# Operands 256 bytes apart within 512, a staging pool beside the first phase, and an early router, in a transformer layer on one core

## The chip, the cores and the metric

The kernel runs on one core of one Trainium2 chip, in one launch. The metric is the device time of that core in microseconds; beside it stands the span, the time between the first and the last instruction of one profiled execution.

## The reference, cut to what matters

Everything is float32, batch 1, 1024 tokens of width 1024. Two blocks follow each other; the first has an attention and convolution mixer and a mixture of experts, the second a recurrent branch (HGRN) and a forgetting attention (FOX).

```
mod = silu(c) @ w_ada + b_ada                     # sh1, sc1, g1, sh2, sc2, g2; the same for the 256 context tokens
xn = rmsnorm(x) * (1 + sc1) + sh1                 # and xn_c of the context
q, k, v, gb, gc, xc = split(xn @ w_in)            # rope on q and k; context keys and values ahead
attn = head_out((softmax(q0 k0) - lam softmax(q1 k1)) @ v)
conv = gb * conv3(gc * xc)
h = x + g1 * rmsnorm(concat(attn, conv) @ w_out)
xn = rmsnorm(h) * (1 + sc2) + sh2
aff = softmax(xn @ w_router)                      # 16 experts
g, idx = top_k(aff.T, 128)                        # each expert takes its 128 best tokens
ff = scatter_add(idx, (silu(xn[idx] @ w_gate) * (xn[idx] @ w_up)) @ w_down * g)
h = h + g2 * rmsnorm(ff)
# second block: u = rmsnorm(h); y = concat(hgrn(u), fox(u)); h += y @ w_out_2
# h += sigmoid(h @ w_ple_gate_2) * (p @ w_ple_2); out = rmsnorm(h)
```

## The kernel before, in words

Every large product is made of three. A float32 operand is split into a high part, rounded to the type fp32r, and a low part, the rest: ACT casts the high part (L82) and VectorE subtracts (L83). `mm3` then adds high x high, high x low and low x high (L77 to L79). In the rows the operand that streams (the moving one) is named first behind the arrow, the one loaded into the array (the stationary one) second. A product has 128 rows, 128 columns of the stationary operand, and 512 or 256 columns of the moving one.

Tiles lie in pools. A pool is a stretch of each partition's memory; pools of the left side are stacked from the low end, those opened with `side="right"` from the high end, in the order in which they are opened. The place of a tile is therefore the sum of the sizes ahead of it. Nearly all tiles are multiples of 512 bytes; a few small ones (`sg`, 4 bytes; `idxT` and `gT`, 64 bytes each; `mx`, `sm`, `r` of 24 and 8 bytes; `cu`, 4104 bytes) set the residue of all that lie behind them. By these sums the residues modulo 512 in this kernel are: pools on the right (`xn`, `wo`, `mw`, `uT`, `wk`) 480; `cx` and `pw` (context and qkv weights) 224; in attention K, Q and V 224, a 0 and the conv weights 32; in the output projection `mh` and `ml` 96; the MoE's `xs`, hidden rows and `ml`, HGRN's and FOX's `pj`, and the last projection's `finw`, `finy` and `finl` 352.

The work follows in stages, by the profile: modulation and the projections to q, k, v (to 268 us); attention, with the convolution's products between its steps (to 578); the output projection with the router, `phase2` and `mixed` (to 694); the experts' choice of tokens (to 775); the MoE (to 1360); the second block's normalization, HGRN, FOX and the last projection.

In `phase0`, eight blocks of `w_ada` of 1 MB come through three buffers of `pw`; VectorE accumulates the first 512 columns over the context's and the tokens' vector, PE makes the rest. `A1` (L213) ends this. Then 256 context tokens and two groups of 512 tokens are normalized, transposed, and written as `ch`/`cl`, `xn[0]` and `xn[1]`. `qkv` opens the pool `pA` only after `phase0`'s pool `p0` is closed, so its tiles (`cos`, `sin`, the staging tiles `sth` and `stl`, and rope's) lie where `p0` lay, and the first instruction to use such a tile waits for those that used the place before.

In `phase2`, `mixed` runs for eight blocks of 128 tokens: output projection, two RMS norms (`rstd` is Ln and Exp on ACT), then `xn` by two operations on VectorE (L613, L614), eight transposes, logits, softmax into `af`. The first MoE weight blocks are loaded during this (`next_raw`). `ple` follows, a small product for the end, then `choose`: 16 rounds of MAX8, FIND_INDEX8 and MATCH_REPLACE8 over the affinities. The MoE's weights come as 192 blocks of 1 MB; `block` casts and splits them in order into `mw` (four of six) or `ml` (two of six). The first `PB` = 4 are subtracted on POOL, `NR` = 6 raw buffers are in flight. A scheduler sets the order of each engine's instructions when the program is built, by priority and free tiles, and each engine then executes its own in that order; `issue_after` in the change adds a bound to it.

```
hi, lo = self.block()
for k in range(2):
    for n in range(2):
        matmul(ps[n], xh[:, i, :], hi[:, k, c])   # stationary, moving
```

Of the kernel before, what the change touches and what calls it, by code (L numbers as in the profile page):

```python
# [19 lines left out]
P = 128  # L20
D = 1024
# [28 lines left out]
class Kernel:  # L50
# [16 lines left out]


# [22 lines left out]
    def constants(self, st):  # L91
# [18 lines left out]
        self.sg = self.t(c, [P, 1], F32, "sg")  # L110
# [20 lines left out]
    def phase0(self):  # L131

        nc, I = self.nc, self.I
        with ExitStack() as st:
# [4 lines left out]
            def load(src, r0):  # L139
                x = self.t(p, [P, D], F32, "x", bufs=7)  # L140
                nc.sync.dma_start(x, src[r0:r0 + P, :])
                xs.append(x)

            def wa(cb, kh):
                w = self.t(self.pw, [P, 4, 512], F32, "raw", bufs=3)
                nc.sync.dma_start(w, I["w_ada"][0, kh * 512:(kh + 1) * 512, cb * 512:(cb + 1) * 512].rearrange("(k p) c -> p k c", p=P))
# [3 lines left out]
            order = ((1, 0), (0, 0), (1, 1), (2, 0), (0, 1), (2, 1), (3, 0), (3, 1))  # L150
# [3 lines left out]
            for b in range(2):  # L154
                load(I["ctx"][0], b * P)
# [10 lines left out]
            nc.vector.tensor_tensor(self.sc.rearrange("p k v -> p v k"), e, cv, op=ALU.mult)  # L166
# [3 lines left out]
            nc.vector.tensor_tensor(pr, lvv[:, :, 0, :], lvv[:, :, 1, :], op=ALU.mult)  # L170
# [8 lines left out]
            tm = self.t(self.pp, [P, 512], F32, "mm", bufs=4)  # L179
            acc = [self.t(p, [P, 512], F32, f"acc{v}") for v in range(2)]  # L180
            ps = None
            for i, (cb, kh) in enumerate(order):
                w = was[i]
                if i + 3 < len(order):
                    was.append(wa(*order[i + 3]))
                if cb == 0:
                    for k in range(4):
                        for v in range(2):
                            s = self.sc[:, kh * 4 + k, v:v + 1]
                            if kh + k == 0:  # L190
                                nc.vector.tensor_scalar(acc[v], w[:, k, :], s, None, op0=ALU.mult)
                            else:
                                nc.vector.scalar_tensor_tensor(acc[v], w[:, k, :], s, acc[v], op0=ALU.mult, op1=ALU.add)
                    if kh == 0:
                        continue
                    for j in range(4):
                        for v in range(2):
                            nc.tensor.matmul(tm[:, 2 * j + v:2 * j + v + 1], acc[v][:, j * P:(j + 1) * P], self.onec, start=True, stop=True)
                    continue
                if kh == 0:  # L200
                    ps = self.t(self.pp, [P, 512], F32, "mm", bufs=4)
                for k in range(4):
                    nc.tensor.matmul(ps[:2, :], self.sc[:, kh * 4 + k, :], w[:, k, :], start=(kh * 4 + k == 0), stop=(kh * 4 + k == 7))
                if kh == 1:
                    m2 = self.t(p, [2, 512], F32, "m2", bufs=2)
                    nc.vector.tensor_copy(m2, ps[:2, :])
                    for j in range(4):
                        c = 2 * (cb * 4 + j)
                        nc.tensor.transpose(tm[:, c:c + 2], m2[:, j * P:(j + 1) * P], self.ident[:2, :2])
            md = self.t(p, [P, 16, 2], F32, "md")  # L210
            nc.vector.tensor_tensor(md, tm[:, :32].rearrange("p (j v) -> p j v", v=2), VC[:, 16:32].unsqueeze(2).broadcast_to([P, 16, 2]), op=ALU.add)
            nc.vector.tensor_copy(self.SH1, md[:, 0:8, :])
            nc.vector.scalar_tensor_tensor(self.A1, md[:, 8:16, :], 1.0, VC[:, 32:40].unsqueeze(2).broadcast_to([P, KB, 2]), op0=ALU.add, op1=ALU.mult)  # L213

            raws = [self.wraw(512, kh) for kh in range(2)]
            for b in range(8):
                load(I["x"][0], b * P)
            for v, g, blks in ((1, 0, xs[0:2]), (0, 0, xs[2:6]), (0, 1, xs[6:10])):
# [7 lines left out]
                for k in range(KB):  # L226
                    tp = self.t(pp, [P, 512], F32, "tp", bufs=3)
                    for b, x in enumerate(blks):
                        nc.tensor.transpose(tp[:, b * P:(b + 1) * P], x[:, k * P:(k + 1) * P], self.ident)
                    tt = self.t(p, [P, 512], F32, "tt", bufs=2)  # L230
                    nc.scalar.activation(tt[:, :n], tp[:, :n], AF.Identity, scale=self.A1[:, k, v:v + 1], bias=self.SH1[:, k, v:v + 1])
                    hi, lo = (self.ch, self.cl) if v else self.xn[g]
                    if k % 2:
                        nc.scalar.copy(hi[:, k, :], tt[:, :n])
                    else:
                        nc.vector.tensor_copy(hi[:, k, :], tt[:, :n])
                    nc.vector.tensor_tensor(lo[:, k, :], tt[:, :n], f(hi[:, k, :]), op=ALU.subtract)
                if v:
                    self.W = [self.wsplit(r) for r in raws]


    def phase1(self):
        nc, I = self.nc, self.I
        with ExitStack() as st:
            self.stx = ExitStack()
            xp = self.pool(self.stx, "xn", side="right")
            self.xn = [(self.t(xp, [P, KB, 512], F32R, f"xh{g}"), self.t(xp, [P, KB, 512], F32R, f"xl{g}")) for g in range(2)]
            with ExitStack() as st2:
# [3 lines left out]
                self.pw = self.pool(st2, "pw")  # L252
                self.pp = self.pool(st2, "pAp", 2, space=PSUM)
# [4 lines left out]
    def qkv(self, st):  # L258
# [5 lines left out]
        self.cos = self.t(w, [P, SEQ], F32, "cos")  # L264
        self.sin = self.t(w, [P, SEQ], F32, "sin")
        nc.sync.dma_start(self.cos, I["k_cos"])
        nc.sync.dma_start(self.sin, I["k_sin"])
        wsl = lambda W, c: [(W[k // 4][0][:, k % 4, c], W[k // 4][1][:, k % 4, c]) for k in range(KB)]
        groups = ((0, CTX, (self.ch, self.cl)), (CTX, 512, self.xn[0]), (CTX + 512, 512, self.xn[1]))
        for base, dst in ((512, self.K_d), (0, self.Q_d)):  # L270
            W = self.W if base else self.win(0)
            for c0, n, x in groups[0 if base else 1:]:
                for h in range(HEADS):
# [3 lines left out]
                    hi = self.t(w, [P, 512], F32R, "sth", bufs=2)  # L277
                    lo = self.t(w, [P, 512], F32R, "stl", bufs=2)
# [8 lines left out]
            if base:  # L287
                W = self.win(1024)
                for b in range(10):
# [3 lines left out]
                    hi = self.t(w, [P, 512], F32R, "sth", bufs=2)  # L293
                    lo = self.t(w, [P, 512], F32R, "stl", bufs=2)
# [13 lines left out]
    def wraw(self, c0, kh):  # L308
        raw = self.t(self.pw, [P, 4, 512], F32, "raw", bufs=3)
# [44 lines left out]
    def rope(self, ps, t0, scale, hi, lo):  # L354

        nc, w = self.nc, self.wp
# [54 lines left out]
    def scores(self, i):  # L411
        nc, w, pp = self.nc, self.wp, self.pp
        h, b = divmod(i, 8)
        if b == 0:
# [18 lines left out]
        mx = self.t(w, [P, 2, 3], F32, "mx", bufs=3)  # L433
        sm = self.t(w, [P, 2, 3], F32, "sm", bufs=3)
# [54 lines left out]
    def conv(self, cb, which, g, w, bufs, early=False):  # L489
        nc = self.nc  # L490
        if which == 0 and g == 0:
            u = self.t(w, [P, SEQ + 2], F32, "cu", bufs=1)
# [5 lines left out]
        if g == 0:  # L498
            def tile(dt, tag):
                if not early:  # L500
                    return self.t(w, [P, KB, P], dt, tag, bufs=2)
                return self.t(self.pw, [P, 4, 512], dt, tag, bufs=3)[:, 0:2, :].rearrange("p a (b c) -> p (a b) c", c=P)
# [37 lines left out]
    def phase2(self):  # L540

        nc, I = self.nc, self.I
        with ExitStack() as st:
# [8 lines left out]
            affT = self.t(w, [2 * NE, 512], F32, "affT")  # L552
            self.raws = []
# [6 lines left out]
            for i in range(8):  # L560
# [24 lines left out]
    def mixed(self, w, pp, tb, wo, G1, SH2, A2, wr, af):  # L585
# [27 lines left out]
        nc.vector.scalar_tensor_tensor(xn, x, s2[:, 3:4], A2, op0=ALU.mult, op1=ALU.mult)  # L613
        nc.vector.tensor_tensor(xn, xn, SH2, op=ALU.add)  # L614
        nc.scalar.dma_start(self.xn2_d[t, :], xn)
        xT = self.t(w, [P, KB, P], F32, "xT", bufs=1)
        for kh in range(2):
            tp = self.t(pp, [P, 512], F32, "tp")
            for k in range(4):
                nc.tensor.transpose(tp[:, k * P:(k + 1) * P], xn[:, (kh * 4 + k) * P:(kh * 4 + k + 1) * P], self.ident)  # L620
# [4 lines left out]
        r4 = self.t(w, [P, 4], F32, "r4", bufs=2)  # L625
        nc.vector.tensor_reduce(r4[:, 0:1], lg[:, :NE], axis=AX.X, op=ALU.max)
        nc.vector.tensor_scalar(r4[:, 1:2], r4[:, 0:1], -1.0, None, op0=ALU.mult)
        nc.scalar.activation(af, lg[:, :NE], AF.Exp, bias=r4[:, 1:2], accum_out=r4[:, 2:3])
        nc.vector.reciprocal(r4[:, 3:4], r4[:, 2:3])
        nc.vector.tensor_scalar(af, af, r4[:, 3:4], None, op0=ALU.mult)  # L630
# [84 lines left out]
    def block(self):  # L715
# [5 lines left out]
        return self.hlrows(self.mw if (self.nb - 1) % 6 < 4 else self.ml, raw, self.nc.gpsimd if self.nb <= PB else None)  # L721
# [503 lines left out]
    def fox_scores(self, h, tb):  # L1225
# [28 lines left out]
        sm = self.t(w, [P, 2], F32, "sm", bufs=6)  # L1254
# [244 lines left out]
```

## Time and profile before

| what | value |
|---|---|
| median of 3 runs | 2869.68 us (2868.32 to 2872.84) |
| the profiled execution | 2866.51 us, span 2864.7 us |
| mean granted clock | 0.967 |
| PE busy | 2645.4 us (92%), 14213 matmuls |
| VectorE (DVE) busy | 2002.0 us (70%) |
| ScalarE (ACT) busy | 1624.9 us (57%) |
| GpSimd (POOL) busy | 247.7 us (9%) |
| DMA | 516.43 MB, mean 180 GB/s |

A matmul's busy time covers its passage through the array, and the next one starts before it ends; the distance from start to start tells what one costs in a dense row. A releaser in brackets ("4.22 <-DVE stl L83") gives the idle time of the engine ahead of an instruction and what ended it.

### The profile page before, as it was taken

The page shows a single profiled execution, that of the slowest core. Times are in us where ns is not written, and L with a number is a line of the kernel's source. Part 1 is how long each engine was busy: PE and PEld are TensorE (multiplying, and loading weights), DVE is VectorE, ACT ScalarE, POOL GpSimd, SP SyncE. Part 2 cuts the span into 40 slices and gives each one's busy share as a digit, 9 for nine tenths or more (in the row PEclk, how much of TensorE's full clock was granted, in tenths as well). Part 3 has the DMA queues.
Part 4 walks back from the last instruction along what each step waited for, and adds up shares of the span by engine and source line. Part 5 has one row for each costly group of instructions (what it writes and reads, how often), then busy time and mean ns, then how long its engine had stood idle before and what let it go on. Part 6 is the DMA issues. An engine that isn't in the chain of part 4 may idle for free.

```text
span 2864.7 us, 38667 instructions
## 1 busy us (share of the span) xinstructions
PE 2645.4 (92%) x14213; PEld 2205.3 (77%) x14213; DVE 2002.0 (70%) x3287; ACT 1624.9 (57%) x2858; POOL 247.7 (9%) x344
## 2 busy tenths in 40 slices
PE   7899999887699999999599999998999998989998
PEld 3677887776588877777489999997878786777776
DVE  5864998845688888887557767673777676776535
ACT  5212898734377777776545545543666665774335
POOL 0101000003000000000100000000111110230000
PEclk9999999998799999999799999999999999999999
DMA  7767333256399999998612122226665766475612
GB/s 283 233 208 197 94 87 90 71 189 228 144 373 375 365 365 370 368 354 280 231 46 52 45 44 46 38 72 161 177 162 139 164 161 139 136 192 190 201 59 81
DMA packets 309090, 516.43 MB, mean 180 GB/s; under 512 B 52529, under 2 KB 180094, under 8 KB 308900
## 3 DMA queue, kind: packets, MB, share of 16 engines
q1 hardware_dynamic: 291628, 456.04, 51.3%
q0 software_dynamic: 11136, 36.25, 4.4%
q10 hardware_dynamic: 6136, 21.67, 2.0%
q8 instruction: 112, 1.84, 0.3%
q14 instruction: 78, 0.64, 0.1%
HBM read 421.01 MB, written 92.88 MB: 179 GB/s over the span
## 4 chain that ended last, share of the span: by engine, by line
PE 54%; DMA 7%; ACT 6%; DVE 3%; issue 2%; SPq 0%; POOL 0%; DVEq 0%; ACTq 0%; POOLq 0%
PE mm L77 9%; PE mm L79 9%; PE mm L78 9%; PE av L1300 2%; PE pu L732 2%; PE pu L733 2%; PE pu L731 2%; PE pg L732 2%; PE py L732 2%; PE py L733 2%; PE py L731 2%; PE pg L733 2%; PE pg L731 2%; PE sc L1021 2%; PE tp L1291 1%
## 5 line engine op out<-in xcount | busy, mean ns | idle before, releaser
L83 DVE TENSOR_TENSOR wlo<-raw,whi 128x2048 fp32r<-128x2048 f32 (+1 forms) x280 | 542.0, 1963 | 167.5 <-ACT whi L82 163.6
L82 ACT CAST whi<-raw 128x2048 fp32r<-128x2048 f32 (+1 forms) x284 | 459.4, 1653 | 142.3 <-PE mm L78 65.2
L77 PE MATMUL mm<-uh,whi 128*128 128x512 f32 x640 | 258.6, 404 | 0.9 <-ACT uh L793 0.9
L78 PE MATMUL mm<-ul,whi 128*128 128x512 f32 x640 | 256.2, 400 | 0.0
L79 PE MATMUL mm<-uh,wlo 128*128 128x512 f32 x640 | 255.3, 399 | 0.0
L79 PE MATMUL mm<-whi,ul 128*128 128x256 f32 x768 | 220.5, 287 | 0.0
L77 PE MATMUL mm<-whi,uh 128*128 128x256 f32 x768 | 220.2, 287 | 0.0
L78 PE MATMUL mm<-wlo,uh 128*128 128x256 f32 x768 | 217.6, 283 | 0.0
L77 PEld LDWEIGHTS mm<-whi,uh 128*128 128x128 f32 x768 | 145.4, 189 | 0.2
L79 PEld LDWEIGHTS mm<-whi,ul 128*128 128x128 f32 x768 | 145.5, 189 | 0.1
L78 PEld LDWEIGHTS mm<-wlo,uh 128*128 128x128 f32 x768 | 145.3, 189 | 0.2
L1269 ACT ACTIVATE lg<-lg,sm 128x128 f32<-128x128 f32 (+7 forms) x128 | 99.5, 777 | 80.4 <-DVE sm L1268 79.7
L79 PEld LDWEIGHTS mm<-uh,wlo 128*128 128x128 f32 x640 | 121.8, 190 | 26.1
L77 PEld LDWEIGHTS mm<-uh,whi 128*128 128x128 f32 x640 | 121.9, 191 | 24.7 <-ACT uh L793 1.4
L442 ACT ACTIVATE e<-sc,mx 128x512 f32<-128x512 f32 (+1 forms) x192 | 118.3, 626 | 39.1 <-DVE mx L441 38.2
L78 PEld LDWEIGHTS mm<-ul,whi 128*128 128x128 f32 x640 | 122.2, 191 | 23.7
L77 PE MATMUL mm<-xh,whi 128*128 128x512 f32 x320 | 128.6, 402 | 5.6 <-DVE stl L83 4.2
L79 PE MATMUL mm<-xh,wlo 128*128 128x512 f32 x320 | 127.2, 397 | 0.0
L78 PE MATMUL mm<-xl,whi 128*128 128x512 f32 x320 | 126.9, 397 | 0.0
L1300 PE MATMUL av<-pT,V 128*128 128x256 f32 x640 | 109.5, 300 | 18.1 <-ACT pT L82 13.3
L1300 PEld LDWEIGHTS av<-pT,V 128*128 128x128 f32 x640 | 92.6, 198 | 41.2 <-ACT pT L82 31.1
L1265 DVE SCALAR_TENSOR_TENSOR lg<-sc,FT,nF 128x512 f32<-128x512 f32 (+3 forms) x160 | 91.7, 583 | 40.5 <-PE sc L1262 28.1
(386 smaller groups left out, 6997.7 us busy)
## 6 DMA issues: line engine op xcount, KB each, us to landing
raw<-in_w_gate_dram SPq DMA_DIRECT2D x64, 1024.0 KB
raw<-in_w_up_dram SPq DMA_DIRECT2D x64, 1024.0 KB
raw<-in_w_down_dram SPq DMA_DIRECT2D x64, 1024.0 KB
raw<-in_w_in_dram SPq DMA_DIRECT2D x76, 512.0 KB
wada<-in_w_ada_dram SPq DMA_DIRECT2D x32, 512.0 KB
Q<-Q_d SPq DMA_DIRECT2D x64, 256.0 KB
yraw<-yT_d SPq DMA_DIRECT2D x22, 512.0 KB
raw<-in_w_ada_dram SPq DMA_DIRECT2D x8, 1024.0 KB
```

The costliest lines, as they stand in the source:

```text
L77: self.nc.tensor.matmul(ps, ah, bh, start=(i == 0), stop=False)
L78: self.nc.tensor.matmul(ps, ah, bl, start=False, stop=False)
L79: self.nc.tensor.matmul(ps, al, bh, start=False, stop=(i == n - 1))
L82: self.nc.scalar.copy(hi, src)
L83: (eng or self.nc.vector).tensor_tensor(lo, src, f(hi), op=ALU.subtract)
L442: nc.scalar.activation(e[:, c0:c0 + n], ps[:, :n], AF.Exp, scale=-1.0, bias=mx[:, m, c:c + 1], accum_out=sm[:, m, c:c + 1])
L731: self.nc.tensor.matmul(ps[n], xh[:, i, :], hi[:, k, c], start=(i == 0), stop=False)
L732: self.nc.tensor.matmul(ps[n], xh[:, i, :], lo[:, k, c], start=False, stop=False)
L733: self.nc.tensor.matmul(ps[n], xl[:, i, :], hi[:, k, c], start=False, stop=(i == KB - 1))
L1265: nc.vector.scalar_tensor_tensor(lg[:, c0:c0 + full], ps[:, :full], Ft, nF[:, c0:c0 + full], op0=ALU.subtract, op1=ALU.add)
L1269: nc.scalar.activation(lg[:, :n], lg[:, :n], AF.Exp, scale=-1.0, bias=sm[:, 0:1], accum_out=sm[:, 1:2])
L1300: nc.tensor.matmul(ps[:, :256], V[:, k, :], pT[k // 4][j][:, k % 4, :], start=(k + j == 0), stop=(k == nkb - 1 and j == 1))
```

## The change

It adds small pads and rounds small tiles up, so that the places of tiles move; it opens a pool `pS` (`self.ws`) for the staging, rope, cos and sin tiles ahead of `phase0`, loads `w_ada` as eight blocks of rows into a pool of their own on the right, and accumulates block by block; it moves the hi copies of `phase0` to VectorE; the router works on x·A2 before rstd is known and multiplies afterwards, with SH2's logits made once (`routed`); the first six weight blocks of the MoE are ordered behind the last softmax; and `ple`'s low part goes to POOL. The lines "..." leave out what is repeated or only renamed.

```diff
+    def pad(self, st, n, **kw):
+        p = self.pool(st, self.nm("pad"), **kw)
+        self.nc.gpsimd.memset(self.t(p, [P, n], F32, "pad"), 0.0)
...
-        self.sg = self.t(c, [P, 1], F32, "sg")
+        self.sg = self.t(c, [P, 16], F32, "sg")[:, 0:1]
...
+            sta = ExitStack()
+            ap = self.pool(sta, "ada", side="right")
+            def wa(k):
+                w = self.t(ap, [P, 2 * D], F32, "wa", bufs=KB)
+                nc.sync.dma_start(w, I["w_ada"][0, k * P:(k + 1) * P, 0:2 * D])
+                return w
+            acc = self.t(p, [P, D], F32, "x", bufs=6).rearrange("p (v c) -> p v c", v=2)
-            was = [wa(*order[i]) for i in range(3)]
+            was = [wa(k) for k in range(5)]
+            for b in range(2):
+                load(I["ctx"][0], b * P)
+            was += [wa(k) for k in range(5, KB)]
+            raws = [self.wraw(512, kh) for kh in range(2)]
+            for b in range(3):
+                load(I["x"][0], b * P)
+            self.cos = self.t(self.ws, [P, SEQ], F32, "cos")
+            self.sin = self.t(self.ws, [P, SEQ], F32, "sin")
...
+            for k, w in enumerate(was):
+                for v in range(2):
+                    s = self.sc[:, k, v:v + 1]
+                    if k == 0:
+                        nc.vector.tensor_scalar(acc[:, v, :], w[:, 0:512], s, None, op0=ALU.mult)
+                    else:
+                        nc.vector.scalar_tensor_tensor(acc[:, v, :], w[:, 0:512], s, acc[:, v, :], op0=ALU.mult, op1=ALU.add)
+                for cb in range(3):
+                    nc.tensor.matmul(ps[cb][:2, :], self.sc[:, k, :], w[:, (cb + 1) * 512:(cb + 2) * 512], start=(k == 0), stop=(k == KB - 1))
...
+            sta.close()
+            xp = self.pool(self.stx, "xn", side="right")
...
-                    if k % 2:
-                        nc.scalar.copy(hi[:, k, :], tt[:, :n])
-                    else:
-                        nc.vector.tensor_copy(hi[:, k, :], tt[:, :n])
+                    nc.vector.tensor_copy(hi[:, k, :], tt[:, :n])
...
+                self.ws = self.pool(st2, "pS")
-                    hi = self.t(w, [P, 512], F32R, "sth", bufs=2)
-                    lo = self.t(w, [P, 512], F32R, "stl", bufs=2)
+                    hi = self.t(self.ws, [P, 512], F32R, "sth", bufs=2)
+                    lo = self.t(self.ws, [P, 512], F32R, "stl", bufs=2)
-        raw = self.t(self.pw, [P, 4, 512], F32, "raw", bufs=3)
+        raw = self.t(self.pw, [P, 4, 512], F32, "raw", bufs=2)
-        nc, w = self.nc, self.wp
+        nc, w = self.nc, self.ws
...
+        mx = self.t(w, [P, 2, 3], F32, "mx", bufs=4)
+        sm = self.t(w, [P, 2, 3], F32, "sm", bufs=4)
-        r = self.t(w, [P, 2], F32, "r", bufs=3)
+        r = self.t(w, [P, 2], F32, "r", bufs=8)
-            u = self.t(w, [P, SEQ + 2], F32, "cu", bufs=1)
+            u = self.t(w, [P, SEQ + P], F32, "cu", bufs=1)
...
+            self.rb = self.t(w, [P, 64], F32, "rb")[:, :NE]
+            nc.scalar.copy(self.rb, self.routed(w, pp, SH2, wr)[:, :NE])
...
+                self.lastaf = af[0:1, i % 2, 0:1]
-                    nc.vector.tensor_copy(affT[:, (i // 2) * P:(i // 2 + 1) * P], tp[:2 * NE, :P])
+                    self.lastT = nc.vector.tensor_copy(affT[:, (i // 2) * P:(i // 2 + 1) * P], tp[:2 * NE, :P])
...
-        nc.vector.scalar_tensor_tensor(xn, x, s2[:, 3:4], A2, op0=ALU.mult, op1=ALU.mult)
-        nc.vector.tensor_tensor(xn, xn, SH2, op=ALU.add)
+        nc.vector.tensor_tensor(xn, x, A2, op=ALU.mult)
+        lg = self.routed(w, pp, xn, wr)
+        nc.vector.scalar_tensor_tensor(af, lg[:, :NE], s2[:, 3:4], self.rb, op0=ALU.mult, op1=ALU.add)
+        nc.vector.scalar_tensor_tensor(xn, xn, s2[:, 3:4], SH2, op0=ALU.mult, op1=ALU.add)
         nc.scalar.dma_start(self.xn2_d[t, :], xn)
...
+        self.last = nc.scalar.activation(af, af, AF.Exp, bias=r4[:, 1:2], accum_out=r4[:, 2:3])
...
+            self.pad(st, 64)
-        return self.hlrows(self.mw if (self.nb - 1) % 6 < 4 else self.ml, raw, self.nc.gpsimd if self.nb <= PB else None)
+        pool = self.mw if (self.nb - 1) % 6 < 4 else self.ml
+        if self.nb > NR:
+            return self.hlrows(pool, raw)
+        with ExitStack() as st:
+            st.enter_context(self.tc.issue_after(self.last.ins))
+            if self.nb > PB:
+                st.enter_context(self.tc.issue_after(self.lastT.ins))
+                return self.hlrows(pool, raw)
+            if self.nb > 1:
+                st.enter_context(self.tc.issue_after(self.opened.ins))
+                return self.hlrows(pool, raw, self.nc.gpsimd)
+            hi, lo = [self.t(pool, list(raw.shape), F32R, x) for x in ("whi", "wlo")]
+            self.opened = self.nc.gpsimd.tensor_copy(lo[0:1, 0, 0:1], self.lastaf)
+            self.split(raw, hi, lo, self.nc.gpsimd)
+            return hi, lo
...
+            sm = self.t(w, [P, 2], F32, "sm", bufs=8)
-            self.split(tp[:, :256].rearrange("p (k t) -> p k t", k=2), xh, xl)
+            nc.scalar.copy(x, tp[:, :256])
+            self.split(x.rearrange("p (k t) -> p k t", k=2), xh, xl, nc.gpsimd)
+            self.pad(st, 120, side="right")
-            self.idxT = self.t(self.rowp, [P, NE], I32, "idxT")
-            self.gT = self.t(self.rowp, [P, NE], F32, "gT")
+            self.idxT = self.t(self.rowp, [P, 64], I32, "idxT")[:, :NE]
+            self.gT = self.t(self.rowp, [P, 64], F32, "gT")[:, :NE]
```

## Rows read from the trace of the kernel before

**Rows 1.** Busy time by stretch: us, engine busy, PEclk, DMA share, GB/s.

```profile
15.00:43.00 28.00, 22.94 (x78) 6.80 (x78) 14.45 (x23) 8.71 (x17) 0.00 (x0) 1.00 0.93 333
...
80.00:144.00 64.00, 61.33 (x249) 48.01 (x250) 54.75 (x88) 9.96 (x13) 13.68 (x8) 0.97 0.76 248
...
578.00:694.00 116.00, 108.34 (x536) 89.30 (x535) 53.46 (x80) 42.94 (x109) 4.28 (x7) 0.96 0.57 194
...
775.00:1360.00 585.00, 569.26 (x2560) 460.37 (x2560) 476.58 (x282) 414.72 (x315) 43.61 (x29) 1.00 0.97 352
```

**Rows 2.** Timeline of PE in V's projection: start us, us, engine, line, operation, out<-in.

```profile
153.00 0.39 PE L77 MATMUL mm<-whi,xh 128*128 128x512 f32 x1
...
159.80 0.39 PE L77 MATMUL mm<-whi,xh 128*128 128x512 f32 x1
```

**Rows 3.** Timeline of PE in the MoE.

```profile
913.60 0.39 PE L731 MATMUL pg<-whi,xsh 128*128 128x512 f32 x1
...
919.04 0.40 PE L731 MATMUL pu<-whi,xsh 128*128 128x512 f32 x1
...
924.40 0.40 PE L733 MATMUL pu<-whi,xsl 128*128 128x512 f32 x1
```

**Rows 4.** Timeline of PE in the last projection.

```profile
2647.87 0.40 PE L77 MATMUL mm<-w2h,yh 128*128 128x512 f32 x1
...
2662.51 0.39 PE L77 MATMUL mm<-w2h,yh 128*128 128x512 f32 x1
...
2673.27 0.40 PE L79 MATMUL mm<-w2h,yl 128*128 128x512 f32 x1
...
2751.52 0.39 PE L79 MATMUL mm<-w2h,yl 128*128 128x512 f32 x1
```

**Rows 5.** Timeline of PE in attention's logits.

```profile
404.15 0.41 PE L439 MATMUL sc<-K,Q 128*128 128x512 f32 x1
...
404.40 0.39 PE L440 MATMUL sc<-K,Q 128*128 128x512 f32 x1
```

**Rows 6.** Groups of instructions: busy us, mean ns, idle before.

```profile
L77 PE MATMUL mm<-uh,whi 128*128 128x512 f32 x640 | 258.6, 404 | 0.9 <-ACT uh L793 0.9
...
L77 PE MATMUL mm<-whi,uh 128*128 128x256 f32 x768 | 220.2, 287 | 0.0
```

**Rows 7.** Timeline of the start, DVE and PE.

```profile
40.71 0.17 DVE L213 SCALAR_TENSOR_TENSOR A<-md,VC 128x16 f32<-128x16 f32 x1
...
65.85 0.69 DVE L237 TENSOR_TENSOR xl<-tt,xh 128x512 fp32r<-128x512 f32 x1 [0.49 <-ACT xh L234]
...
79.97 0.80 PE L77 MATMUL mm<-xh,whi 128*128 128x512 f32 x1 [4.22 <-DVE stl L83]
```

**Rows 8.** Timeline of ACT, POOL and DVE behind the last output projection.

```profile
677.84 1.22 DVE L614 TENSOR_TENSOR xn<-xn,row 128x1024 f32<-128x1024 f32 x1
...
693.54 0.60 ACT L601 ACTIVATE tmp<-mm 128x512 f32<-128x512 f32 x1 [2.53 <-PE mm L79]
...
696.16 19.88 POOL L83 TENSOR_TENSOR wlo<-raw,whi 128x2048 fp32r<-128x2048 f32 x4 [3.79 <-ACT whi L82]
...
697.07 1.90 ACT L82 CAST whi<-raw 128x2048 fp32r<-128x2048 f32 x1
...
699.44 0.75 DVE L606 SCALAR_TENSOR_TENSOR tmp<-mm,s,row 128x512 f32<-128x512 f32 x1
...
701.40 4.84 DVE L607 TENSOR_TENSOR x<-x,tmp 128x1024 f32<-128x1024 f32 x1
...
722.97 0.17 DVE L626 TENSOR_REDUCE r<-lg 128x1 f32<-128x16 f32 x1 [5.86 <-PE lg L624]
...
726.57 0.68 DVE L641 MAX8 vi<-affT 32x8 f32<-32x512 f32 x1
```

**Rows 9.** Timeline of POOL and DVE in FOX.

```profile
2402.67 2.40 POOL L1245 TENSOR_TENSOR Gd<-nF,cmask 128x1024 f32<-128x1024 f32 x1 [9.77 <-DMA nF<-F_d]
...
2402.90 0.55 DVE L1268 TENSOR_REDUCE sm<-lg 128x1 f32<-128x384 f32 x1
```

More of the change, by code (lines that the diff above doesn't have):

```diff
@@ L165, in phase0 @@
             nc.vector.reciprocal(e, e)
-            nc.vector.tensor_tensor(self.sc.rearrange("p k v -> p v k"), e, cv, op=ALU.mult)
+            self.cos = self.t(self.ws, [P, SEQ], F32, "cos")
+            self.sin = self.t(self.ws, [P, SEQ], F32, "sin")
+            nc.sync.dma_start(self.cos, I["k_cos"])
+            nc.sync.dma_start(self.sin, I["k_sin"])
+            silu = nc.vector.tensor_tensor(self.sc.rearrange("p k v -> p v k"), e, cv, op=ALU.mult)
+            tm = self.t(self.pp, [P, 512], F32, "mm", bufs=4)
@@ new lines, in phase0 @@
+            ps = [self.t(self.pp, [P, 512], F32, "mm", bufs=4) for cb in range(3)]
+            for k, w in enumerate(was):
[7 more added lines that the diff above has]
+                    nc.tensor.matmul(ps[cb][:2, :], self.sc[:, k, :], w[:, (cb + 1) * 512:(cb + 2) * 512], start=(k == 0), stop=(k == KB - 1))
@@ new lines, in phase0 @@
+            for cb in range(3):
+                m2 = self.t(p, [P, 512], F32, "tt", bufs=2)[:2, :]
+                (nc.scalar.copy if cb % 2 else nc.vector.tensor_copy)(m2, ps[cb][:2, :])
+                for j in range(4):
+                    c = 2 * (cb * 4 + 4 + j)
+                    nc.tensor.transpose(tm[:, c:c + 2], m2[:, j * P:(j + 1) * P], self.ident[:2, :2])
+            for j in range(4):
+                for v in range(2):
+                    nc.tensor.matmul(tm[:, 2 * j + v:2 * j + v + 1], acc[:, v, j * P:(j + 1) * P], self.onec, start=True, stop=True)
@@ L168, in phase0 @@
+            load(I["x"][0], 3 * P)
             pr = self.t(p, [P, 2, 64], F32, "pr")
             lvv = lv.rearrange("p (a b) d -> p a b d", b=2)
-            nc.vector.tensor_tensor(pr, lvv[:, :, 0, :], lvv[:, :, 1, :], op=ALU.mult)
+            with self.tc.issue_after(silu.ins):
+                nc.vector.tensor_tensor(pr, lvv[:, :, 0, :], lvv[:, :, 1, :], op=ALU.mult)
             l2 = self.t(p, [P, 2], F32, "l2")
@@ L177, in phase0 @@
             nc.vector.tensor_scalar(self.sg, VC[:, 68:69], 1.0 - LAM_INIT, None, op0=ALU.mult)
[L179 to L191, printed above, removed]
-                            else:
[L193 to L217, printed above, removed]
@@ L218, in phase0 @@
-            for v, g, blks in ((1, 0, xs[0:2]), (0, 0, xs[2:6]), (0, 1, xs[6:10])):
+            for v, g, b0, b1, nxt in ((1, 0, 0, 2, 6), (0, 0, 2, 6, 8), (0, 1, 6, 10, 8)):
+                blks = xs[b0:b1]
                 n = len(blks) * P
@@ L232, in phase0 @@
                     hi, lo = (self.ch, self.cl) if v else self.xn[g]
-                    if k % 2:
-                        nc.scalar.copy(hi[:, k, :], tt[:, :n])
-                    else:
-                        nc.vector.tensor_copy(hi[:, k, :], tt[:, :n])
+                    nc.vector.tensor_copy(hi[:, k, :], tt[:, :n])
                     nc.vector.tensor_tensor(lo[:, k, :], tt[:, :n], f(hi[:, k, :]), op=ALU.subtract)
+                for b in range(len(xs) - 2, nxt):
+                    load(I["x"][0], b * P)
                 if v:
@@ L292, in qkv @@
                     self.mm3(ps, [((x[0][:, k, t0:t0 + P], x[1][:, k, t0:t0 + P]), (W[k // 4][0][:, k % 4, :], W[k // 4][1][:, k % 4, :])) for k in range(KB)])
-                    hi = self.t(w, [P, 512], F32R, "sth", bufs=2)
-                    lo = self.t(w, [P, 512], F32R, "stl", bufs=2)
+                    hi = self.t(self.ws, [P, 512], F32R, "sth", bufs=2)
+                    lo = self.t(self.ws, [P, 512], F32R, "stl", bufs=2)
                     self.split(ps, hi, lo)
@@ L501, in tile @@
                     return self.t(w, [P, KB, P], dt, tag, bufs=2)
[L502 removed]
+                return self.t(self.pw, [P, 4, 512], dt, tag, bufs=2 if dt is F32 else 3)[:, 0:2, :].rearrange("p a (b c) -> p (a b) c", c=P)
             c0 = (2048, 2560, 1536)[which] + cb * P
@@ L624, in mixed @@
             nc.tensor.matmul(lg[:, :NE], xT[:, k, :], wr[:, k, :], start=(k == 0), stop=(k == KB - 1))
[L625 to L630, printed above, removed]
+        return lg
     def choose(self, w, pp, affT):
```

33 lines of the change are left out of this document (16 added, 17 removed).

## The prediction

> **What bounds the kernel.** I read first the busy time by stretch of the span. PE is the engine to look at: it is busy 569.26 of 585 us in the MoE and 108.34 of 116 us in the output projection, with DVE at 476.58 and 53.46 [rows 1]. What PE does there is nearly all 512-column matmuls back to back, so the next view is PE's timeline, and in it the distance from one start to the next, since the durations overlap. Three readings:
>
> - V's projection: 30 intervals from 153.00 to 159.80, 226.7 ns each [rows 2].
> - the MoE: 24 intervals from 913.60 to 919.04, 226.7 ns, and then, from one line of the program to the next and with nothing else changed, 23 intervals from 919.04 to 924.40, 233.0 ns [rows 3].
> - the last projection: 63 intervals from 2647.87 to 2662.51, 232.4 ns, and 345 from 2673.27 to 2751.52, 226.8 ns, under the same names and shapes [rows 4].
>
> So a dense 512-column matmul has two prices about 6 ns apart. I worked out where each operand lies in its partition, from the sizes of the tiles allocated ahead of it (the section on the kernel gives the residues modulo 512 bytes). Take d, the moving operand's residue less that of the stationary operand loaded while it streams. V has d = 256 and costs 226.7. The first MoE stretch takes its weights from `ml`, d = 0, and costs 226.7; the second takes them from `mw`, d = 128, and costs 233.0. In the last projection the weights come first from `wk` (d = 128, 232.4) and then from `finw` (d = 0, 226.8). Every dense pair follows this: d = 0 or 256 is cheap, any other dear. The clock is at its upper level in the MoE, 2.4 GHz (1.00 granted) for both prices [rows 1], so the clock isn't the difference.
>
> Two stretches are not bound by PE's streaming. At the start K's matmuls on the tokens begin at 79.97 though the last piece of `xn[0]` was written at 65.85 + 0.69 = 66.5; what releases them is an `stl` split on DVE [rows 7]. Behind the last output projection 33.0 us pass between the first square (693.54) and the first MAX8 (726.57) [rows 8].
>
> **Padding.** The right pad is 480 bytes, so `xn`, `wo`, `mw`, `uT` and `wk` move from 480 to 0; `sg` at 64 bytes and the grown `idxT`, `gT`, `rb`, `mx`/`sm`, `r`, `cu` and the MoE pad bring the left operands to 0 or 256. By my sums of sizes d becomes 0 or 256 for: attention's conv matmuls 18 x 24 = 432; the output projection 8 x 2 x 24 = 384; the MoE's `mw` blocks, two thirds of 2304 = 1536; those with `uT` moving 3 x 640 = 1920 (640 is the count of one of the three products [rows 6]); `out_part` 3 x 80 = 240; the last projection's `wk` part 528. Together 5040. At 232.9 - 226.8 = 6.1 ns in the midst [rows 3, 4] that is 30.7 us. Not all of it comes through: where DVE or ACT paces PE, a shorter matmul only lengthens a wait. PE is busy 0.97 of the MoE and 0.93 of the output projection [rows 1]; for the mix I take 0.8, which is 24.5 us. The 768 `ml` products in the MoE go from d = 0 to 256; by V's row [rows 2] that costs nothing.
>
> The 256-column matmuls change their d too (768 x 3 with the weight moving [rows 6], and 1120 products with V). No row tells their price by d. An operand read for half as long could be dearer by half of 6.1, 3 ns, so the bound is 3 ns on 3424, 10 us either way; I take nothing, since some pairs come from a dear d and others from a cheap one. Bounds of the padding: 10 (half comes through, the narrow ones lose) to 35.
>
> The padding's cost: memsets of 64 to 120 columns on an idle POOL, and two or three kilobytes of the partition; nothing.
>
> **Start.** The same 8.39 MB of `w_ada` and 1.05 MB of `ctx` must land before A1 (40.71 [rows 7]). They came at 333 GB/s with the DMA engines 0.93 busy [rows 1]; issued together, without waits for three buffers, at most 333 / 0.93 = 358 GB/s, which saves 28.3 - 26.4 = 2 us, and the chain behind the last block is shorter (three products and one accumulation per block, spread): 2 to 4 in all, A1 near 37. From A1 to `xn[0]` took 66.5 - 40.7 = 25.8 us; the x blocks and K's weights now land earlier, so I put `xn[0]` at 61. K's staging (`sth`, `stl`, rope tiles, cos and sin) leaves `pA`, which lies over phase 0's tiles and can be used only when `xn[1]` is done, for a pool of its own. So K on `xn[0]` starts near 61 in place of 79.97: gross 19, 17 to 24 by how early the loads let it be. What moves in: `xn[1]`'s DVE work, which filled the 13.5 us before 79.97, now runs beside K's ropes, where DVE was busy 54.75 of 64 us [rows 1], 9 us of room; and eight hi copies of 512 columns go from ACT to DVE at about the 0.69 us of the split beside them [rows 7]. That returns 3 to 8; I take 4 with the loads' share of the gross at 20. Net 16, bounds 8 to 24. cos and sin (1 MB, 2.9 us of DMA) go ahead of x4 to x7, which are wanted some 15 us later: nothing. Raw buffers 3 to 2: hidden under K's matmuls, if they take longer than a 1 MB load.
>
> **Row blocks and early router.** In before, ACT's casts of the MoE's weight blocks (1.90 each) stand among the last block's steps, and POOL's 19.88 us of `wlo` hold up VectorE's two-input operations: the addition at 701.40 takes 4.84, its like at 677.84 took 1.22 [rows 8]. After, casts wait for the last Exp and POOL for the last `af`; the router's transposes and logits work on x·A2 before rstd is known, and SH2's part comes from one product ahead of the loop. Rebuilt without the disturbance: 693.54 to 699.44 is 5.9, less two casts 2.1; to 701.40 is 2.0; addition 1.2; x·A2 1.2; transposes, copies and logits 5.9 (the wait at 722.97); to MAX8 3.6 [rows 8]; 0.2 for the added af. That is 16.2, against 33.0: 17. The square and rstd of x run beside the 5.9. With ple's `pxl` splits leaving DVE, 1 more: 18.
>
> Next late is the MoE's first product: the casts it wants (four at 1.9, 7.6 us) now run behind the Exp, and `wlo` (19.9) on POOL, while the choice's 16 rounds of three passes at about 0.68 us [rows 8] take 33 us on DVE. Cover is there: 20 + 2 < 33. A MAX8 has one SBUF input, and beside POOL's 2.40 us operation in FOX a one-input reduction of 384 columns kept 0.55 us [rows 9]. The gathers queue behind `wlo` and ple's `pxl` on POOL; 20 + 8 x 0.6 (a quarter of 2.40 for a quarter of the columns [rows 9]) still ends before the indices. The router on SH2 ahead of the loop takes the same 5.9 us once, hidden where PE waits for the first `mh` to be loaded and split; 5.9 if not. Bounds 5 to 22.
>
> **Sum.** 24.5 + 16 + 18 = 58.5 off the profiled execution's 2866.51 (span 2864.7): 2808. The median of the runs shown is 3.2 above that execution: 2869.68 - 58.5 = 2811.
>
> **Rivals.** (A) The residue isn't the cause, and the two prices belong to the pools for another reason (which tags rotate, what ACT writes meanwhile). Then padding gives nothing: 2869.7 - 34 = 2836. Against it: four unrelated pool pairs sort by d [rows 2 to 4]. The Trainium skill's "TensorE: Matmul & The Clock Gate", section "Step-by-step: what each phase is for", speaks for it: TensorE reads the streamed operand and the weights through two independent ports, so "Loading the next tile's weights doesn't steal SBUF read bandwidth from the running matmul." By that the place of the weights could not matter. The 6 ns between rows of equal shape speak against it. Chance 0.08.
>
> (B) DVE eats the start: PE starts at 61 but waits for ropes, and only 0 to 3 us are left: 2869.7 - 42.5 = 2827. For it: 54.75 of 64 us busy [rows 1]. Chance 0.09.
>
> (C) The tail's gain goes to the MoE's start: the choice ends 17 us earlier, but ple's matmuls, the casts or POOL hold the first gather or the PSUM banks: 2869.7 - 40.5 = 2829. Chance 0.06.
>
> (D) Slower: with every operand on two residues, PE's reads meet those of ACT, DVE and the DMA writes, which then also lie on these residues. The one dear pair with d = 0 is in attention's logits, where two products start 0.25 us apart [rows 5]. If all 5040 cost 250 instead of 233, that is 17 ns x 5040 = 86 us, less 34: 2922. It decides from 240 ns on (6.8 ns x 5040 = 34). Against it: V, `ml` and `finw` run dense at these residues beside busy engines at 226.7. Chance 0.05.
>
> **Numbers.** Forecast 0.72, A 0.08, B 0.09, C 0.06, D 0.05. What this kernel's measurement can tell from no change is 0.2%, 5.7 us. D gives slower 0.05; same 0.02 is left for A with B and C together; the rest, 0.93, is faster. Range: the bounds of the three parts don't fall together; from 2784 (35 + 24 + 22, nearly) to 2845, where A with a part of B lies. Predicted 2811.
>
> **What would show it.** Dense 512-column starts at 226 to 228 ns in `pu`, `uh` and `wk` products: padding right; at 233, A; above 240, D. K on `xn[0]` starting at 57 to 63 and ending its stretch 13 to 20 us earlier: the start right; starting there and stalling, B. First MAX8 16 to 18 us behind the last square, and the MoE's first product some 18 us earlier relative to that square: the tail right; if only the first holds, C. The forecast fails most likely in how much of the matmuls' gain PE passes on, above all in the stretch with `uT`, where DVE and ACT are busy too.

## The result, and the profile after

The changed kernel takes 2838.94 us (median of 4 runs, 2836.00 to 2841.59) against 2871.26 for the kernel before: ratio 0.9885, 95% interval 0.9869 to 0.9901, 32.3 us faster. Beside the experiments it was timed once more: 2845.43 against 2875.66, ratio 0.9889 (0.9872 to 0.9907). Forecast were 58.5 us; the time lies in the range, near its upper end. The profiled execution has a span of 2837.3 us.

The stretches of the changed kernel that answer to [rows 1] (us, busy time of PE, PEld, DVE, ACT, POOL, PEclk, DMA share, GB/s):

```profile
15.00:43.00 28.00, 19.36 (x59) 4.76 (x57) 10.91 (x15) 11.81 (x23) 0.00 (x0) 0.91 0.98 393
75.00:139.00 64.00, 61.38 (x273) 48.50 (x274) 60.29 (x99) 16.32 (x24) 12.12 (x10) 1.00 0.65 218
573.00:690.00 117.00, 113.03 (x580) 95.11 (x579) 56.27 (x90) 45.11 (x115) 4.27 (x7) 0.97 0.56 191
753.60:1336.60 583.00, 563.91 (x2560) 461.66 (x2560) 480.68 (x284) 417.15 (x317) 45.26 (x29) 0.99 0.96 356
```

DVE is now busy 60.29 of 64 us beside K's first products, where it was 54.75. PE's timeline in the MoE, from a `pg` product with weights in `mw`, through two blocks in `ml`, on to a `pu` product with weights in `mw` again, which answers to [rows 3]:

```profile
892.53 0.39 PE L762 MATMUL pg<-whi,xsh 128*128 128x512 f32 x1
...
902.73 0.39 PE L762 MATMUL pu<-whi,xsh 128*128 128x512 f32 x1
```

45 intervals in 10.20 us: 226.7 ns each, with no step where the pool changes. In the last projection the part with weights from `wk`, which answers to the first pair of [rows 4]:

```profile
2598.87 0.39 PE L82 MATMUL mm<-w2h,yh 128*128 128x512 f32 x1
...
2614.96 0.39 PE L84 MATMUL mm<-w2h,yl 128*128 128x512 f32 x1
```

71 intervals in 16.09 us: 226.6 ns where it was 232.4. So the padding does what it was forecast to do to a product. The start, DVE's and PE's timeline, which answers to [rows 7]:

```profile
31.69 0.68 DVE L199 COPY tt<-mm 2x512 f32<-2x512 f32 x1 [7.00 <-PE mm L196]
...
34.96 2.29 DVE L88 TENSOR_TENSOR wlo<-raw,whi 128x2048 fp32r<-128x2048 f32 x1 [0.53 <-ACT whi L87]
...
37.96 9.36 DVE L194 SCALAR_TENSOR_TENSOR x<-wa,sc,x 128x512 f32<-128x512 f32 x14
...
51.40 0.17 DVE L209 SCALAR_TENSOR_TENSOR A<-md,VC 128x16 f32<-128x16 f32 x1
...
74.94 0.50 PE L82 MATMUL mm<-xh,whi 128*128 128x512 f32 x1 [0.39 <-DVE stl L88]
```

The first of these products starts at 74.94 in place of 79.97, not at 61: A1 comes at 51.40, 10.7 us later than before. The accumulations over the blocks of `w_ada` (14 of 16 in the row of 37.96) stand as one block behind a copy that waits for PE's last product and behind a wide low-part split, though DVE was idle 7.00 us ahead of that copy. Behind the last output projection, which answers to [rows 8], and on to the MoE's start:

```profile
689.64 0.60 ACT L608 ACTIVATE tmp<-mm 128x512 f32<-128x512 f32 x1 [1.36 <-PE mm L84]
...
707.62 0.68 DVE L656 MAX8 vi<-affT 32x8 f32<-32x512 f32 x1
...
743.31 0.21 DVE L660 CAST vi<-idx 32x128 f32<-32x128 uint32 x1
...
746.91 0.31 PE L663 MATMUL tp<-ident,vi 32*128 32x32 f32 x2
...
750.88 1.07 ACT L1372 COPY po<-mm 128x512 f32<-128x512 f32 x2 [2.72 <-DMA ple_d<-po]
...
752.35 3.70 ACT L87 CAST whi<-raw 128x2048 fp32r<-128x2048 f32 x2 [0.40 <-ACT po L1372]
...
756.59 0.80 PE L762 MATMUL pg<-whi,xsh 128*128 128x512 f32 x1 [1.06 <-ACT xsh L87]
...
760.79 1.22 PE L764 MATMUL pg<-whi,xsl 128*128 128x512 f32 x2 [1.70 <-DVE xsl L88]
```

In the kernel before, the first product of the MoE was this one:

```profile
777.17 0.80 PE L731 MATMUL pg<-whi,xsh 128*128 128x512 f32 x1
```

The first MAX8 comes 18.0 us behind the square, where it took 33.0 and 16.2 were forecast, and the first product of the MoE 66.9 us behind it, where it took 83.6. But the chosen indices lie ready at 743.5 and PE transposes them only at 746.91, and ACT's casts of two weight blocks come at 752.35, behind the copies of `ple`, each of which waits for a store. The product at 760.79 then waits for a split on DVE.

### The profile page after: what moved, and what is told of

It is laid out like the page before. It is cut to its first block, busy times and chain, and to the rows that moved or that the text cites. A ratio compares the mean times of both kernels' runs of the same rounds, so it can differ in the third digit from the quotient of the medians.

```text
span 2837.3 us, 38733 instructions
## 1 busy us (share of the span) xinstructions
PE 2638.5 (93%) x14237; PEld 2221.2 (78%) x14237; DVE 1995.0 (70%) x3298; ACT 1620.8 (57%) x2858; POOL 247.6 (9%) x355
## 4 chain that ended last, share of the span: by engine, by line
PE 72%; DMA 10%; ACT 8%; DVE 6%; issue 3%; SPq 1%; POOL 0%; DVEq 0%; ACTq 0%; POOLq 0%
PE mm L82 13%; PE mm L84 12%; PE mm L83 12%; PE av L1333 2%; PE pu L763 2%; PE pu L764 2%; PE pu L762 2%; PE py L764 2%; PE py L763 2%; PE py L762 2%; PE pg L763 2%; PE pg L764 2%; PE sc L1052 2%; PE pg L762 2%; PE tp L1324 1%
```

## Experiments

Ratios are to the kernel before, timed beside each, with 95% intervals. Where times are subtracted directly, the two kernels ran on the same chip; where ratios are subtracted, the intervals of both count, some 7 us either way together. The runs of other residues have no ratio. "Excess" is worked out from the starts in a trace: the distance to the next start less 227 ns (512 columns) or 118 ns (256), summed where it is below 15 ns, so without waits and without the lower clock.

**The parts alone.** `pads_only` is the kernel before with the pads and rounded tiles, `start_only` with phase 0's changes and the pool `pS`, `tail_only` with `routed`, `block` and `ple`.

> The kernel before with the pads and rounded tiles alone. Theory 1: the dense 512-column products all fall to 227 ns, but only the stages that PE paces pass it on; summed over the stages of the changed kernel's trace that is about 16 us (attention 4, MoE 8, second block's normalization 2, last projection 2, FOX and HGRN nothing): ratio 0.9945, with FOX as long as before. Theory 2: the padding gives the 24.5 us of the forecast, ratio 0.9915, and the two other parts lose some 8 us of it. Theory 3: the padding is not what made the products faster: ratio 1.000 and dense starts still at 233.

> The kernel before with the new start alone (blocks of w_ada by rows, own pools, staging beside the first phase). Theory 1: A1 comes 10 us later than before, since the accumulations run as one block behind the wide low-part split, and eats what the staging pool gives: within 2 us of before, ratio 0.9995 to 1.0005. Theory 2: the start gives the 16 us of the forecast and loses them only beside the padding: ratio 0.9945.

> The kernel before with the early router, the ordered weight blocks and ple's low part on POOL alone. Theory 1: the first MAX8 comes 15 us earlier behind the last square, and the MoE's start gives back some 3 to 4 of it (cold clock, late casts): 11 to 13 us, ratio 0.9957. Theory 2: all of the forecast's 18 us arrives: ratio 0.9937.

Measured: pads 2854.00, ratio 0.9916 (0.9899 to 0.9934); start 2872.28, 0.9986 (0.9975 to 0.9998); tail 2865.55, 0.9960 (0.9946 to 0.9975). By its own runs each part gains. The start gave 4 us of 16, nearer theory 1, and the tail 11.5 of 18, which is theory 1. The pads' ratio stands with theory 2, some 24 us; the spans of the profiles do not decide, since that of `pads_only` (2851.7) is 13.0 us below the first of the kernel before and 20.0 below a second (2871.7). Added up the three parts give 39.5 us, more than the 32 of the change; the intervals together allow for that difference, and it is not explained further. The next run measures the padding in the changed kernel.

**The changed kernel without its pads**, and the kernel before and the changed one again:

```diff
-            self.pad(st, 120, side="right")
-            self.pad(st, 64)
-        self.sg = self.t(c, [P, 16], F32, "sg")[:, 0:1]
+        self.sg = self.t(c, [P, 1], F32, "sg")
...
-        r = self.t(w, [P, 2], F32, "r", bufs=8)
+        r = self.t(w, [P, 2], F32, "r", bufs=3)
...
```

> The changed kernel without its pads and rounded tiles (start and tail kept). Theory 1 (the padding is worth 16 to 18 us, stage by stage): 2855 against the changed kernel's 2839 beside it, a difference of 15 to 19. Theory 2 (it is worth the forecast 24.5): a difference of 23 to 26. Dense starts of `mw` products back at 233 by both.

> The changed kernel, beside the others. By every theory 0.9885 of before within 0.002.

> The kernel before, unchanged, profiled beside the others, to see how far the stages differ from one profile to the next. Expected by every theory: MoE 581, HGRN 530, FOX 628 us within 1 us each; the projections to q, k and v up to 3 us longer than the 188 of the first profile.

Measured: without pads 2865.54, ratio 0.9966 (0.9953 to 0.9979); the changed kernel 2845.43; the kernel before, in its one profiled run, 2873.51. The padding edit is worth 20.1 us, between the two theories. Start and tail together are worth 0.34%, 10 us of the 34 forecast.

The stages' lengths from first and last matmul (us):

| stage | before | before again | no pads | changed | changed again | pads only |
|---|---|---|---|---|---|---|
| K on `xn[0]` to attention | 188.2 | 190.7 | 193.0 | 192.1 | 195.6 | 191.3 |
| attention | 317.5 | 316.4 | 317.4 | 313.6 | 312.2 | 311.8 |
| output projection | 107.9 | 109.1 | 110.7 | 109.0 | 108.8 | 106.9 |
| MoE | 584.9 | 585.4 | 590.0 | 583.0 | 582.7 | 576.7 |
| FOX | 628.4 | 628.5 | 633.1 | 629.1 | 632.3 | 628.6 |

FOX took 627.6 to 629.1 us in nine of the fourteen profiles and 632 to 638 in five, with no edit in common; what does that stays open, and one profile alone tells no difference below 5 us. One thing the edit does besides moving places: `mx`, `sm` and `r` get more buffers (3 to 4, 3 to 8), and the scheduler another order in attention. Attention is 5.2 us shorter with the pads than without, while its 512-column products account for 1.05 us (below); no run separates the rest from the places.

**Accumulations first.** The changed kernel with this, and with the fourth token block's square behind four of the context's activations on ACT:

```diff
-                        nc.vector.scalar_tensor_tensor(acc[:, v, :], w[:, 0:512], s, acc[:, v, :], op0=ALU.mult, op1=ALU.add)
+                        last = nc.vector.scalar_tensor_tensor(acc[:, v, :], w[:, 0:512], s, acc[:, v, :], op0=ALU.mult, op1=ALU.add)
...
-                (nc.scalar.copy if cb % 2 else nc.vector.tensor_copy)(m2, ps[cb][:2, :])
+                with self.tc.issue_after(last.ins):
+                    nc.vector.tensor_copy(m2, ps[cb][:2, :])
...
-                    self.W = [self.wsplit(r) for r in raws]
+                    with self.tc.issue_after(last.ins):
+                        self.W = [self.wsplit(r) for r in raws]
```

> The changed kernel with the 16 accumulations ordered ahead of the copies and of the wide low-part splits on DVE, the three copies on DVE, and the fourth token block's square behind four of the context's activations on ACT. Theory 1 (the late block of accumulations cost the start its gain): A1 near 38 in place of 51.4, K on xn[0] 10 to 13 us earlier, and the time 10 to 12 us below the changed kernel's, ratio to before 0.985. Theory 2 (DVE's work beside K's ropes eats it, whatever A1 does): K starts earlier but ends its stretch at the same time; ratio 0.988 as the changed kernel.

Measured: 2835.76, ratio 0.9852 (0.9836 to 0.9868), which lies 0.0037 or 10.6 us below the changed kernel's ratio of 0.9889. Its DVE timeline:

```profile
25.52 9.36 DVE L194 SCALAR_TENSOR_TENSOR x<-wa,sc,x 128x512 f32<-128x512 f32 x14
...
40.94 2.28 DVE L88 TENSOR_TENSOR wlo<-raw,whi 128x2048 fp32r<-128x2048 f32 x1
...
43.22 0.17 DVE L210 SCALAR_TENSOR_TENSOR A<-md,VC 128x16 f32<-128x16 f32 x1
```

A1 comes at 43.22, 8.2 us earlier than in the changed kernel, but not near the 38 of theory 1 and still behind the 40.71 of the kernel before: the accumulations still run as one block, and a wide split stands ahead of A1. K on `xn[0]` starts at 64.92 in place of 74.94, which is theory 1. Attention starts at 260.32, earlier by 6.7 us than in the changed kernel's first profile (266.99) and by 9.4 than in its second (269.70), so a share for theory 2 is not shown. What the moved square and the moved copy do by themselves was not tried.

**Two output tiles for `ple`**, on top of that; `ple`'s products copy their result into one tile `po`, stored before the next copy may begin:

```diff
-            o = self.t(w, [P, D], F32, "po", bufs=1)
+            o = self.t(w, [P, D], F32, "xn", bufs=2)
```

> The kernel of the accumulations first, and besides ple's output tile in two buffers (the free tiles of xn) in place of one. Theory 1 (the MoE's start gives time back because ACT's casts of blocks 5 and 6 stand behind ple's copies, each of which waits for the store of the one ahead): the casts end before the choice does, the first MoE products come some 3 us earlier, and the time is 2 to 4 us below that of accumulations first, ratio to before 0.984. Theory 2 (what the MoE's start gives back is the clock at its lower level after the choice): no difference, 0.985.

> Accumulations first and two output tiles, once more, beside the run with the odd copies on ACT. By every theory 0.9816 of before within 0.002.

Measured: 2823.81, ratio 0.9816 (0.9799 to 0.9833), and again 2821.97, 0.9813 (0.9796 to 0.9831): 21.6 us below the changed kernel timed beside the first. The second tile alone is worth 10 us by the ratios (0.9852 to 0.9816), more than theory 1 had. The traces agree: from the output projection's last product to the MoE's last pass 646.9 us in the run of accumulations first, and 637.9 and 637.1 in the two profiles with the second tile. The timeline of the first of these at the end of the choice:

```profile
733.07 0.22 DVE L667 CAST vi<-idx 32x128 f32<-32x128 uint32 x1
...
733.40 0.30 PE L670 MATMUL tp<-ident,vi 32*128 32x32 f32 x2
...
736.92 3.70 ACT L87 CAST whi<-raw 128x2048 fp32r<-128x2048 f32 x2 [2.83 <-DMA ple_d<-xn]
...
742.01 0.80 PE L769 MATMUL pg<-whi,xsh 128*128 128x512 f32 x1
```

PE takes the indices 0.33 us after the cast began (1.9 in the second profile), not 3.60; the casts end at 740.6, 1.4 us ahead of the first product, and no product behind it waits for a split, as the one at 760.79 did in the changed kernel. In the kernel before, ACT waited for the store of `po` too (2.26 to 2.74 us, five times), but nothing waited for ACT there: PE took the indices 0.27 us after their cast began. It became the last wait when the choice moved earlier. The clock is at its lower level for the first products here too (1.2 GHz, 0.50 granted from 742 to 746 us; 743.02 to 743.45 is 430 ns for one product). Eight intervals are of that length in this profile and four in the other, ten with accumulations first, so theory 2 accounts for 0.4 to 1.2 us of the difference.

**The odd high copies back on ACT**, on top of that:

```diff
-                    nc.vector.tensor_copy(hi[:, k, :], tt[:, :n])
+                    (nc.scalar.copy if k % 2 else nc.vector.tensor_copy)(hi[:, k, :], tt[:, :n])
```

> Accumulations first and two output tiles, with the odd high copies of the start back on ACT. Theory 1 (DVE paces the projections to q, k and v beside the second group's normalization): the stretch from K's first product on xn[0] to attention gets 2 to 4 us shorter than the 195 of the kernel beside it, and the time with it. Theory 2 (the copies were hidden, or ACT's waits take their place): no difference above 1 us.

Measured: 2818.06, ratio 0.9795 (0.9777 to 0.9812), the fastest kernel here, 57 us below the kernel before beside it (2874.72); against the kernel without this edit beside it 3.9 us, with intervals that overlap. The stretch from K on `xn[0]` to attention, first of this kernel, then of the one beside it:

```profile
62.00:255.60 193.60, 186.93 (x817) 149.37 (x816) 132.21 (x200) 38.86 (x58) 22.62 (x18) 1.00 0.63 206
```

```profile
63.90:260.30 196.40, 187.91 (x814) 150.37 (x813) 133.57 (x204) 35.77 (x52) 23.19 (x18) 0.99 0.62 201
```

It is 2.8 us shorter (1.7 against the other profile of that kernel, 195.3). Two profiles of one and the same kernel differ by 2.5 and 3.5 us in this stretch (table above), so neither theory is shown.

**Other residues.** The changed kernel with other sizes of the right pad, one run each:

```diff
-            self.pad(st, 120, side="right")
+            self.pad(st, 72, side="right")    # right_64; 56 in right_256
```

> The changed kernel with a right pad of 288 bytes in place of 480, so that the right pools lie at 192 modulo 512 and differ from the left ones by 64 (mod 512: 448 or 64). Theory 1 (only 0 and 256 are cheap): `mw`, `uT`, `wo` and `wk` products at 232 to 234 ns, 512-column excess over 227 back at some 25 us, time 15 to 20 us above the changed kernel. Theory 2 (the price grows with the distance from 0 or 256): 228 to 230 ns, 5 us above.

> The changed kernel with a right pad of 224 bytes, so that right and left pools lie on the same residue, 256: d = 0 in place of 256. Theory 1 (0 and 256 are the same): `mw` products at 227 ns and the changed kernel's time within 6 us. Theory 2 (256 apart is what helps, and 0 is as dear as in attention's logits): 235 ns or more, 30 us and more slower.

Measured: 2857.06 with the operands 64 apart, 2852.85 with both on the same residue; the kernel before took 2874.72 beside them, the changed one was not timed there. PE's timeline in the MoE with `mw`'s weights, 64 apart and then on the same residue:

```profile
889.77 0.39 PE L763 MATMUL py<-wlo,hth 128*128 128x512 f32 x1
...
896.07 0.39 PE L763 MATMUL pg<-wlo,xsh 128*128 128x512 f32 x1
```

```profile
886.21 0.39 PE L762 MATMUL py<-whi,hth 128*128 128x512 f32 x1
...
894.14 0.39 PE L764 MATMUL pg<-whi,xsl 128*128 128x512 f32 x1
```

27 intervals in 6.30 us are 233.3 ns; 35 in 7.93 are 226.6. By the price of a product it is theory 1 in both: 0 and 256 are alike, and 64 costs as much as 128. The two dear places still differ: with `mw`'s weights nearly all intervals are 233 to 234 ns at 64, while at 128, in the kernel before, they run from 229 to 238 about the same mean. The excess of the 512-column products is 34.7 us at 64, above the 28.2 of the kernel before, and 5.9 on the same residue. The times fit less well. Against the changed kernel on the other chips 2857.06 is 12 to 18 us above, about as theory 1 has it, but 2852.85 is 7 to 14 above, not within 6. FOX was 5.5 to 8.7 us longer in the second of them than in the changed kernel's profiles, the open question of above; one run each decides no more.

## Why the prediction was right in its direction and half wrong in its size

**Padding, 24.5 forecast, 20.1 measured.** The mechanism held: every pool pair that came to 0 or 256 became cheap. The term was mis-sized. Summed over the trace, the 512-column products' excess fell from 28.2 to 6.2 us: 22.0, not 30.7. 5040 products saved 4.4 ns each rather than 6.1, since the step took a dense neighbour for granted: attention's 432 stand among other products and saved 1.05 us, the 1920 with `uT` moving 7.1. The 256-column products, put at nothing, lost 4.6 us of excess (0.2 to 4.7), inside the bound of 10. That leaves 17.5 us of net excess. The share that comes through, put at 0.8, can't be read from 17.5 against 20.1, because some 4 of attention's 5.2 us are not in its products' excess; without them it is about 0.9. FOX and HGRN passed on almost nothing, as the forecast's last sentence feared; the MoE passed on 7.3 us (590.0 to 582.7) of 8.9.

**Start, 16 forecast, 4 measured.** The step that failed is "the chain behind the last block is shorter (three products and one accumulation per block, spread)". The accumulations were not spread; DVE's order put all of them behind the copies, so A1 came 10.7 us late where 2 to 4 early was forecast. That is the gross term: K on `xn[0]` starts at 74.94, 13.9 us behind the forecast's 61, as A1 is 14.4 behind its 37. The term for what moves in beside K's ropes, put at 4, was right: the stretch from there to attention grew by 3.9 us (188.2 to 192.1; 4.9 by the second profiles). `acc_first` shows that the order is the cause: with it mended, 10.6 us come back, though not all of that need be the accumulations' (its edit also moves a square and a copy). It does not bring the forecast's A1, since the 16 accumulations still take DVE from 24.7 to 34.9 in one piece. The transfer bound was too cautious: the blocks came at 424 GB/s (last rows below), not 358, so it was not the loads that were late. Rival B has the outcome, attention 1.2 us earlier (not at all by the second profiles), but not the cause: PE did not start at 61 and then wait for ropes.

**Tail, 18 forecast, 11.5 measured.** The path to the first MAX8 was right to 2 us (15.0 gained, 16.8 by the terms), and the first product of the MoE came 16.7 us earlier behind the square. The loss lies behind that product: from there to its end the MoE took 580.0 us, where with the pads alone it took 574.9. The step that failed is "Cover is there": POOL's and ACT's work was weighed by its length, not by its place in the queue. The two late casts stand on ACT behind `ple`'s blocks, of which each waits for the store of the one before, and PE has the transposes of the indices behind the same blocks. So the transposes come 3.3 us late, and a product waits for the splits (2.33 us from 758.46 to 760.79). That is part of rival C, with `ple` and not POOL as the holder. The second output tile gives back 9 us and not only the 5 lost in the MoE, for it also brings the indices sooner.

**Rival A** is refuted: the place decides, for `right_64` and `right_256` differ in one pad alone. The Trainium skill's "TensorE: Matmul & The Clock Gate", section "Step-by-step: what each phase is for", says that loading the next weights takes no read bandwidth from the running product. Here a product took 233.3 ns or 226.6 by the distance of the two operands alone; the measurement decides, for these float32 operands at 512 columns. Why the distance matters, and whether the stationary operand that counts is the product's own or the next one, no run shows. **Rival D** is refuted as well: all operands on one residue cost 226.6 and no more.

The sum of the range has a slip: its lower end, 2784, is 5 us below what the three bounds give (2869.7 - 81 = 2789). It changes nothing here.

## What to carry to other kernels

Sort dense products by the distance of moving and stationary operand modulo 512 before explaining their price by pools or names; here, at 512 columns, 0 and 256 were cheap and 64 and 128 dear, and a pad of a few hundred bytes moved a whole stack. When a gain hangs on an engine doing work while data arrives, look at the order that the scheduler gives that engine, not only at its idle time: 10 us hung on 16 instructions placed behind one copy. And when a stage is made to end earlier, the next queue to read is that of side work which used to end in time; a single buffer there cost 9 us, and the profile before showed it only as idle time of an engine that nothing waited for.

## What was not expected of the hardware

Narrow products don't follow the same rule. In the second block's projections the 256-column products lie at d = 256 in the changed kernel and 64 apart in `right_64`; PE's timelines, in this order:

```profile
1699.94 0.28 PE L82 MATMUL mm<-whi,uh 128*128 128x256 f32 x1
...
1703.54 0.28 PE L82 MATMUL mm<-whi,uh 128*128 128x256 f32 x1
```

```profile
1702.06 0.28 PE L84 MATMUL mm<-whi,ul 128*128 128x256 f32 x1
...
1703.76 0.28 PE L84 MATMUL mm<-whi,ul 128*128 128x256 f32 x1
```

30 intervals in 3.60 us are 120.0 ns, 15 in 1.70 are 113.3. That is the best stretch at 64; over all products of this kind with a next start within 133 ns the mean is 117.4 there, 119.8 at 256, 119.7 on the same residue (`right_256`) and 119.0 at 128 (the kernel before). So the difference is 2 to 3 ns, the other way round than at 512 columns. HGRN, which is made of these, took 530 and 531 us in the two, so it is not passed on there. Why the sign turns with the width was not tried.

The transfers of the start came faster than in any row of [rows 1]; two stretches of 10 us of the changed kernel (columns as above):

```profile
10.00:20.00 10.00, 10.00 (x20) 1.78 (x19) 0.00 (x0) 0.00 (x0) 0.00 (x0) 1.00 1.01 424
20.00:30.00 10.00, 10.00 (x29) 2.34 (x27) 1.51 (x2) 3.18 (x8) 0.00 (x0) 1.00 1.02 420
```

Blocks of `w_ada` with rows of 8 KB, issued together, moved at 420 GB/s and more, where blocks with rows of 2 KB through three buffers had moved at 333 with the engines 0.93 busy [rows 1]. No run changed one without the other, but the packets in the traces speak for both: one of 2 KB took 94 ns on average from 15 to 43 us of the kernel before (84 at the median), one of 8 KB 309 ns from 10 to 30 us of the changed kernel, 18% less for each byte; the rest goes with the engines' busy share, 1.01 in place of 0.93.
